# A mixed attention and gMLP trunk whose instructions are recorded and put in order by a model of the queues

## The chip, the cores and the metric

The kernel runs on one core of a Trainium2 chip. The metric is the device time of one execution in microseconds (us), lower is better. The core has engines that each work through a queue of their own strictly in order: TensorE (PE, with its weight loads shown apart as PEld), VectorE (DVE), ScalarE (ACT), GpSimd (POOL) and SyncE (SP), which here only starts transfers. An instruction at the head of a queue that waits for another engine holds up all that stand behind it.

## What is computed

One step of a four-layer trunk over 128 context tokens and 256 latent tokens (384 together), 2048 wide, in float32. Each layer is

```
x += gate * W_out( mixer(RMSNorm(x) * (1 + scale) + shift) * silu(z) )
(shift, scale, gate) = silu(cond) @ W_ada + b_ada
```

Layers 0 and 3 mix by windowed attention (16 heads of 128, 4 key heads), layer 1 by neighbourhood attention (16 heads with their own keys), layer 2 by a gMLP with 128x128 mixing in 16 groups. The attention layers also return their context keys and values.

## The kernel before

The large products are float32 products made of three: each operand is split into a high part (`H`, `hH`) and a remainder (`L`, `hL`), and `mm3` or `a_unit` issues H·hH, H·hL and L·hH into one PSUM bank. A weight block of 512 KB (`raw`, four buffers) is fetched by SP, ACT writes its `H` (three buffers), DVE its `L` (three buffers); that is `split`, line 159. One such block is a unit: `a_unit` has 24 products of 384 columns, `b_unit` 18 of 512 columns. 13,824 of the 16,872 products of the program are of these two kinds; the rest below calls them the long or main products.

Between them stand the short ones. `head` (line 812) handles one attention head: it turns q with six transposes (`trR`, 128 columns), forms the scores with three or so products of 128 columns and several of 256 or 384, and turns the probabilities with fourteen transposes before their product with the values. `k_gen` turns the keys. `pe_ada_unit` (line 1161) multiplies the modulation weights (`w_ada`) on PE in four column groups; the part of the modulation that DVE computes is `ada_one`, two reductions of 1024 columns a block (`vttr`, line 135).

The order in each queue is the order in which the Python code calls the engines. Where the main stream has finished a unit, `bg()` (line 302) lets generators advance by one step: a head, the square sums of q and k (`q_gen`, line 783), the next part of the modulation. So a step's transposes stand in the PE queue in a row, six to thirteen of them, and what a step does on DVE or ACT stands in one piece in their queues. The code keeps sums of estimated engine times (`pe_t`, `dve_t`, `act_t`), by which it decides whether a background step fits. `startup` (line 1211) interleaves the modulation of layer 0 with the first products.

Of the kernel before, what the change touches and what calls it, by code (L numbers as in the profile page):

```python
# [1 line left out]

# [6 lines left out]
F32R = mybir.dt.float32r  # L9
# [5 lines left out]
P = 128  # L15
# [21 lines left out]
    return bass.AP(ap.tensor, ap.offset, a)  # L37


class Net:  # L40
    def __init__(self, tc, pool, psum, dram, a):
        self.tc, self.nc, self.a = tc, tc.nc, a
        self.pe_t = self.dve_t = self.act_t = self.slot_t = 0.0
        self.lr = {}

        def t(name, cols, dt=F32):
            return pool.tile([P, cols], dt, name=name, tag=name)

        self.pool, self.seq = pool, 0
        self.hH, self.hL = t("hH", 16 * T, F32R), t("hL", 16 * T, F32R)  # L50
        self.pm, self.px = list(range(NPAIR)), []
        self.xt = [None] * NXP
        self.raw = [t(f"raw{i}", 1024) for i in range(NR)]
        self.H = [t(f"H{i}", 1024, F32R) for i in range(NH)]
        self.L = [t(f"L{i}", 1024, F32R) for i in range(NL)]
        self.araw = [None, None]
        self.cbc = t("cbc", 2048)
        self.qT = t("qT", 2 * T, F32R)
        self.aux = t("aux", 1536)
        self.junk = t("junk", 1024, BF16)  # L60
        self.ident = t("ident", P)
        self.identR = t("identR", P, F32R)
        self.ones = t("ones", P)
        self.mask = t("mask", 256, F32R)
        self.sel = t("sel", 4)
        self.spad = t("spad", 64)
        self.sT = t("sT", 32)
        self.normg = t("normg", 64)
        self.bada = t("bada", 192)
        self.sink = t("sink", 32)  # L70
        self.gk, self.gq = t("gk", P), t("gq", P)
        self.ada = [t(f"ada{i}", 96) for i in range(2)]
        self.accA = t("accA", 32)
        self.Av = [t(f"Av{i}", 32) for i in range(2)]
        self.st = [t(f"st{i}", 12) for i in range(6)]
        self.st_i = 0
        self.sm = [t(f"sm{i}", 24) for i in range(2)]
        self.cqs = [t(f"cq{i}", 12) for i in range(4)]
        self.c12 = t("c12", 12)
        self.bn = t("bn", 3 * 8 * 6)  # L80
        self.mv = t("mv", 6)
        self.bk = [psum.tile([P, 512], F32, name=f"bk{i}", tag=f"bk{i}") for i in range(8)]
        self.srow = dram.tile([2, D], F32, name="srow", tag="srow")
        self.xs = dram.tile([P, 16 * T], F32, name="xs", tag="xs")
        self.misc = []
        self.headq, self.heads, self.head_gap = [], [], 99
        self.heads_done = 0
        self.convq, self.conv_limit, self.conv_done, self.burst = [], 0, 0, 1
        self.ada_half, self.ada_wait, self.ada_hold = -1, 0, False
        self.units, self.uw, self.ua, self.ur, self.nd, self.pos = [], 0, 0, 0, 0, 0  # L90
        self.r_done = self.r_bank = None
# [341 lines left out]
    def setup(self):  # L433
        nc, a = self.nc, self.a
        self.scratch()
        craw, th = self.arow[:, :32], self.arow[:, 32:64]
        self.dma(craw, a["cT"])
        for i in range(NXP):
            self.xt[i] = self.new(f"pair{NPAIR + i}", 1536)
            self.dma(self.xt[i], a["xT"][:, i * 1536:(i + 1) * 1536])  # L440
        self.dma_upto(10)
        nc.scalar.dma_start(self.sel, a["sel"])
        self.act(th, craw, AF.Tanh, scale=0.5)
        make_identity(nc, self.ident)
        nc.vector.memset(self.ones, 1.0)
        nc.vector.memset(self.c12, -0.5)
        self.vstt(th, th, 1.0, craw, ALU.add, ALU.mult)
        self.vts(self.sT, th, 0.5, None, ALU.mult)
        self.pad_s()
        nc.scalar.dma_start(self.normg, a["normg"])  # L450
        nc.scalar.dma_start(self.bada, a["bada"])
# [929 lines left out]
    def run(self):  # L1381
        self.ada_layer = 0
        self.plan()
        self.setup()
        for l in range(4):
            self.ada_layer = l
            if l:
                self.ada_need(l, 0)
                self.make_A(l, 0, min(8, self.dve_chunks(l)))
            if l in (0, 3):  # L1390
                self.attn_layer(l, "win", l // 3)
            elif l == 1:
                self.attn_layer(l, "nat", 0)
            else:
                self.gmlp_layer(l)


# ---- launch: one core
# [111 lines left out]
```

## Time and profile before

| | us |
|---|---|
| median of 3 runs | 3072.14 |
| lowest, highest | 3071.66, 3074.43 |
| the profiled execution, its own time | 3072.06 |
| its span in the trace | 3070.2 |
| PE busy, weight loads busy | 3032.9, 2771.4 |
| DVE busy, ACT busy | 2174.0, 1271.6 |

The span is the stretch from the first to the last recorded instruction; 1.9 us of the execution's time lie outside of it. A product's recorded end is modelled and overlaps with the next one, so the busy share of PE says little; the distance from one product's start to the next one's says what it takes in the stream. By stage: 0 to 200 us is layer 0's startup, to about 660 us layer 0, to about 1430 us layer 1, to about 2530 us layer 2, and the rest layer 3.

### The profile page before, as it was taken

What the parts mean: (1) busy time and instruction counts of PE and PEld (TensorE: products, weight loads), DVE (VectorE), ACT (ScalarE), POOL (GpSimd) and SP (SyncE); (2) the same over time, 40 slices, a digit from 0 to 9 for tenths busy, and PEclk for the clock granted to TensorE, in tenths of its full rate; (3) what the DMA queues carried; (4) which work ended last, traced back from release to release, by engine and by line L of the source; (5) the groups of instructions that cost most, each with busy time, mean ns of one, the idle gap of its engine ahead of it and who ended that gap; (6) DMA issues with size and microseconds to landing.
All of it is one profiled execution on the core that took longest, in us unless ns stands there. A gap on an engine that the chain in (4) does not pass through costs nothing.

```text
span 3070.2 us, 45356 instructions
## 1 busy us (share of the span) xinstructions
PE 3032.9 (99%) x17616; PEld 2771.4 (90%) x17616; DVE 2174.0 (71%) x3604; ACT 1271.6 (41%) x2322; POOL 51.7 (2%) x29
## 2 busy tenths in 40 slices
PE   7999999999999999999999999999999999999999
PEld 4788899978989898998888999999999998999999
DVE  4478789868788888887988998445355566455654
ACT  4355555354444545534333222222232335455542
POOL 0000000000000000000000000000000000000000
PEclk9999999999999999999999999999999999999999
DMA  9756555976666666677777676444454474333343
GB/s 385 276 192 213 200 165 176 337 252 212 206 205 206 204 214 200 205 243 269 246 242 248 219 254 213 132 131 127 134 165 125 135 251 145 114 103 104 106 128 124
DMA packets 187361, 599.05 MB, mean 195 GB/s; under 512 B 21764, under 2 KB 47620, under 8 KB 187140
## 3 DMA queue, kind: packets, MB, share of 16 engines
q1 hardware_dynamic: 186712, 596.00, 58.3%
q8 instruction: 138, 2.26, 0.3%
q14 instruction: 79, 0.65, 0.1%
q10 hardware_dynamic: 432, 0.13, 0.0%
HBM read 580.31 MB, written 15.75 MB: 194 GB/s over the span
## 4 chain that ended last, share of the span: by engine, by line
PE 94%; DVE 2%; ACT 2%; issue 1%; DMA 1%; POOL 0%; SPq 0%; DVEq 0%; ACTq 0%; POOLq 0%
PE bk L109 92%; PE bk L118 3%; ACT junk L150 1%; DVE L L122 1%; DVE pair L133 1%; ACT H L150 0%; DVE pair L122 0%; POOL cq L165 0%; DMA pair<-i_w_ada 0%; ACT Pt L150 0%; DVE junk L137 0%; DMA pair<-i_xT 0%; DMA raw<-i_win_B 0%; DVE PLT L133 0%; DVE Pt L122 0%
## 5 line engine op out<-in xcount | busy, mean ns | idle before, releaser
L150 ACT ACTIVATE H<-raw 128x1024 fp32r<-128x1024 f32 x640 | 676.2, 1058 | 895.1 <-PE bk L109 805.4
L109 PE MATMUL bk<-hH,H 128*128 128x384 f32 x3072 | 1037.5, 338 | 3.4 <-DVE pair L122 3.4
L109 PE MATMUL bk<-hH,L 128*128 128x384 f32 x3072 | 1027.6, 334 | 0.0
L109 PE MATMUL bk<-hL,H 128*128 128x384 f32 x3072 | 1027.0, 334 | 0.0
L122 DVE TENSOR_TENSOR L<-raw,H 128x1024 fp32r<-128x1024 f32 x640 | 781.6, 1222 | 275.8 <-ACT H L150 267.3
L109 PE MATMUL bk<-L,hH 128*128 128x512 f32 x1536 | 600.9, 391 | 8.9 <-DVE L L122 8.9
L109 PE MATMUL bk<-H,hH 128*128 128x512 f32 x1536 | 607.5, 396 | 0.0
L109 PE MATMUL bk<-H,hL 128*128 128x512 f32 x1536 | 602.0, 392 | 0.3 <-DVE hL L122 0.3
L109 PEld LDWEIGHTS bk<-hH,H 128*128 128x128 f32 x3072 | 576.9, 188 | 13.7 <-issue 6.5
L109 PEld LDWEIGHTS bk<-hL,H 128*128 128x128 f32 x3072 | 577.1, 188 | 0.6
L109 PEld LDWEIGHTS bk<-hH,L 128*128 128x128 f32 x3072 | 576.7, 188 | 0.0
L109 PEld LDWEIGHTS bk<-L,hH 128*128 128x128 f32 x1536 | 289.5, 188 | 66.7 <-DVE L L122 11.0
L109 PEld LDWEIGHTS bk<-H,hL 128*128 128x128 f32 x1536 | 289.3, 188 | 65.3 <-DVE hL L122 3.8
L109 PEld LDWEIGHTS bk<-H,hH 128*128 128x128 f32 x1536 | 289.2, 188 | 64.6 <-issue 6.5
L137 DVE CUSTOM_DVE_ANT_0 junk<-araw,cbc,accA 128x1024 bf16<-128x1024 f32 x240 | 307.5, 1281 | 14.2 <-ACT junk L150 7.9
L137 DVE CUSTOM_DVE_ANT_0 junk<-araw,cbc,bada 128x1024 bf16<-128x1024 f32 x240 | 307.5, 1281 | 10.0 <-ACT junk L150 3.0
L133 DVE SCALAR_TENSOR_TENSOR pair<-bk,ada,pair 128x128 f32<-128x128 f32 x320 | 118.6, 413 | 202.4 <-PE bk L109 202.4
L150 ACT ACTIVATE pair<-bk 128x512 f32<-128x512 f32 (+3 forms) x156 | 86.9, 562 | 195.7 <-PE bk L109 172.4
L150 ACT ACTIVATE PLT<-bk 128x512 fp32r<-128x512 f32 (+2 forms) x63 | 34.0, 563 | 168.4 <-PE bk L118 150.2
L150 ACT ACTIVATE PTH<-bk 128x512 fp32r<-128x512 f32 (+2 forms) x74 | 37.0, 523 | 123.1 <-PE bk L118 87.9
L109 PE MATMUL bk<-pair,qT 128*128 128x384 f32 (+2 forms) x336 | 74.9, 332 | 0.0
L150 ACT ACTIVATE junk<-pair 128x128 bf16<-128x128 f32 x216 | 66.8, 309 | 13.4 <-DVE ada L137 5.9
(151 smaller groups left out, 2150.3 us busy)
## 6 DMA issues: line engine op xcount, KB each, us to landing
araw<-i_w_adaT SPq DMA_DIRECT2D x240, 512.0 KB, 3.8
pair<-i_w_ada SPq DMA_DIRECT2D x96, 512.0 KB, 8.2
raw<-i_win_B SPq DMA_DIRECT2D x96, 512.0 KB, 4.2
raw<-i_nat_B SPq DMA_DIRECT2D x96, 512.0 KB, 4.5
raw<-i_win_O SPq DMA_DIRECT2D x64, 512.0 KB, 3.7
raw<-i_gm_V SPq DMA_DIRECT2D x64, 512.0 KB, 4.6
raw<-i_gm_U SPq DMA_DIRECT2D x64, 512.0 KB, 4.5
raw<-i_gm_Z SPq DMA_DIRECT2D x64, 512.0 KB, 4.5
```

Of the source, the lines that this page charges most:

```text
L109: self.nc.tensor.matmul(out, lhsT, rhs, start=start, stop=stop, **kw)
L118: self.nc.tensor.transpose(out.bitcast(F32R), in_, self.identR)
L122: self.nc.vector.tensor_tensor(out=out, in0=in0, in1=in1, op=op)
L133: self.nc.vector.scalar_tensor_tensor(out=out, in0=in0, scalar=s, in1=in1, op0=op0, op1=op1)
L137: self.nc.vector.tensor_tensor_reduce(out=out, in0=in0, in1=in1, op0=op0, op1=op1, scale=1.0, scalar=scalar, accum_out=acc)
L150: self.nc.scalar.activation(out, in_, f, **kw)
```

## The change

A class `Rec` takes the place of the engine handles: while the kernel's code runs, it only notes each instruction with its operands. For each it finds what must come before it: data dependences by ranges of eight columns of a tile, order alone where both stand on one engine. Main products (those that read `hH` or `hL`) are chained and keep their recorded order, as do the products into one bank. Then `order` lays the instructions out in time by a model: once in recorded order, and three times by a list schedule in which PE takes the earliest recorded product that is ready and the other engines take the one whose result is due first. In that model a product that lasts over 100 ns is long; a weight load takes `LDW` = 108 ns and may begin once the load before it is over and the product before has started, and a product starts `LAG` = 56 ns after its load. Where no time is left for the next load, PE takes a long product before a short one. The real instructions are then issued in order of the modelled start. No product, no sum and no transfer is added or taken away, and the tiles are the same.

```diff
-        self.tc, self.nc, self.a = tc, tc.nc, a
+        self.tc, self.nc, self.a = tc, Rec(tc.nc), a
...
-        make_identity(nc, self.ident)
+        make_identity(nc.real, self.ident)
...
                 self.gmlp_layer(l)
+        self.nc.emit()
...
+    def cost(self, e, op, a, k):
+        n = self.cols(a[0] if a else k["out"])
+        if e == "tensor":
+            if op == "transpose":
+                d = 57
+            elif "tile_position" in k:
+                d = 128
+            elif a[2].dtype == F32R:
+                d = (n + 32) / 2.4 if n > P else 57
+            else:
+                d = max(4 * (n + 16) / 2.4, 224)
+            return d, d + 190
...
+    def add(self, e, op, a, k):
...
+        if e == "tensor" and any(s and s[0] in ("hH", "hL") for s in r):
+            if self.main is not None:
+                order.add(self.main)
+            self.main = i
+        self.ops.append((e, op, a, k))
...
+        self.long.append(d > 100)
...
+    SEM, LDW, LAG = 45, 108, 56
...
+    MARGIN = 250
+
+    def schedule(self, late):
...
+        key = [float(i) if self.eng[i] == 0 else late[i] for i in range(n)]
...
+            i = ready[e][0][1]
+            if e == 0:
+                if load + self.LDW + self.LAG > t and not self.long[i]:
+                    i = min((i for _, i in ready[0] if self.long[i]), default=i)
...
+                load = max(load + self.LDW, last)
+                t = last = max(t, load + self.LAG)
+            if e in (1, 2) and wait[e]:
+                end, hold = t + self.dur[i], None
+                for est, j in wait[e]:
+                    if est < end and late[j] < end and late[j] < late[i] and (hold is None or est < hold):
+                        hold = est
+                if hold is not None:
+                    free[e] = hold
+                    continue
...
+    def order(self, passes=3):
+        start, done = self.in_order()
+        for _ in range(passes):
+            start, done = self.schedule(self.due(start))
+        return sorted(range(len(self.ops)), key=lambda i: (start[i], i))
+
+    def emit(self):
+        for i in self.order():
+            e, op, a, k = self.ops[i]
+            getattr(getattr(self.real, e), op)(*a, **k)
```

Three places show what moves. In the rows below, a number behind a name tells buffers apart, `x4` stands for four equal instructions in a row, and all of the change's instructions carry line 314, since they are issued there.

The first is PE in layer 3, some 130 us before the end, where one head's probabilities (`PLT_792`) are turned into banks 5 and 6, and the product with the values of the head before (`PTH_793` with `pair7`) goes into bank 7. Before:

```order
L109 MATMUL bk2_115<-hL_66,H0_71 128x384
L109 MATMUL bk2_115<-hH_65,L0_74 128x384
L118 MATMUL bk5_118<-identR_82,PLT_792_23153 128x128 x4
L118 MATMUL bk6_119<-identR_82,PLT_792_23153 128x128 x3
L109 MATMUL bk7_120<-PTH_793_23207,pair7_700_20540 128x128
L109 MATMUL bk7_120<-PLT_795_23266,pair7_700_20540 128x128
```

And with the change:

```order
L314 MATMUL bk2_115<-hL_66,H0_71 128x384
L314 MATMUL bk2_115<-hH_65,L0_74 128x384
L314 MATMUL bk5_118<-identR_82,PLT_792_918 128x128 x2
L314 MATMUL bk3_116<-hH_65,H1_72 128x384
L314 MATMUL bk5_118<-identR_82,PLT_792_918 128x128 x2
L314 MATMUL bk3_116<-hL_66,H1_72 128x384
L314 MATMUL bk6_119<-identR_82,PLT_792_918 128x128 x2
L314 MATMUL bk3_116<-hH_65,L1_75 128x384
L314 MATMUL bk6_119<-identR_82,PLT_792_918 128x128
L314 MATMUL bk7_120<-PTH_793_919,pair7_700_826 128x128
L314 MATMUL bk3_116<-hH_65,H1_72 128x384
```

Seven transposes in a row have become pairs with a long product between them. Over the whole program the 1,104 transposes stood in 142 runs of 6 to 13 and now stand in 625 runs, 479 of two and 146 of one. Runs of modulation products were 61 and are 69.

At the same place ACT copies the turned probabilities out of banks 5 and 6 (`PTH`, `PLT`) and takes the exponentials of the next head (`Pt_794`) out of banks 7 and 4. Before:

```order
L150 ACTIVATE hH_65<-pair3_749_21949 128x384
L150 ACTIVATE H2_73<-raw2_69 128x1024
L150 ACTIVATE PLT_795_23266<-bk5_118 128x512
L150 ACTIVATE PLT_795_23266<-bk6_119 128x384
L150 ACTIVATE Pt_794_23221,sm0_104<-bk7_120,sm0_104,cq3_109 128x128
L150 ACTIVATE Pt_794_23221,sm0_104<-bk7_120,sm0_104,cq3_109 128x384
L150 ACTIVATE Pt_794_23221,sm0_104<-bk4_117,sm0_104,cq3_109 128x384
```

With the change:

```order
L314 ACTIVATE H2_73<-raw2_69 128x1024
L314 ACTIVATE PTH_793_919<-bk5_118 128x512
L314 ACTIVATE PTH_793_919<-bk6_119 128x384
L314 ACTIVATE Pt_794_920,sm0_104<-bk7_120,sm0_104,cq3_109 128x128
L314 ACTIVATE Pt_794_920,sm0_104<-bk7_120,sm0_104,cq3_109 128x384
L314 ACTIVATE Pt_794_920,sm0_104<-bk4_117,sm0_104,cq3_109 128x384
L314 ACTIVATE H0_71<-raw3_70 128x1024
L314 ACTIVATE sm0_104<-sm0_104,sink_90 128x3
L314 ACTIVATE PLT_795_921<-bk5_118 128x512
```

The exponentials have moved ahead of the copies of `PLT_795`.

The second place is DVE at the first group of heads in layer 1, where q is normed (`q_gen`): a sum (`st2`), from which POOL forms `cq0`, and twelve multiplications by `cq0`, among the splits (`L0`, `L1`, `L2`) of the main stream's weights. Before:

```order
L122 TENSOR_TENSOR L1_75<-raw2_69,H1_72 128x1024
L127 TENSOR_SCALAR st2_100<-st1_99 128x12
L133 SCALAR_TENSOR_TENSOR pair9_297_6149<-pair9_297_6149,cq0_106,gq_92 128x128 x12
L122 TENSOR_TENSOR L2_76<-raw3_70,H2_73 128x1024
L122 TENSOR_TENSOR pair10_301_6243<-pair9_297_6149,pair12_300_6242 128x512 x3
L122 TENSOR_TENSOR L0_74<-raw0_67,H0_71 128x1024
```

With the change (`ISA` is a modulation reduction and, with one operand, the reading of its sum):

```order
L314 TENSOR_TENSOR L2_76<-raw3_70,H2_73 128x1024
L314 ISA junk_80,accA_95<-araw1_294_420,cbc_77,bada_89 128x1024
L314 ISA accA_95 128x1
L314 TENSOR_TENSOR L0_74<-raw0_67,H0_71 128x1024
L314 TENSOR_SCALAR st2_100<-st1_99 128x12
L314 ISA junk_80,accA_95<-araw0_298_424,cbc_77,bada_89 128x1024
L314 ISA accA_95 128x1
L314 ISA junk_80,accA_95<-araw0_298_424,cbc_77,bada_89 128x1024
L314 ISA accA_95 128x1
L314 TENSOR_TENSOR L1_75<-raw1_68,H1_72 128x1024
L314 SCALAR_TENSOR_TENSOR pair9_297_423<-pair9_297_423,cq0_106,gq_92 128x128 x11
L314 TENSOR_TENSOR L2_76<-raw2_69,H2_73 128x1024
```

Two reductions and a split have come between the sum and the multiplications, and the two splits that stood behind the multiplications stand ahead of the sum. The other three groups of the layer are alike.

The third place is SP at the very start, where it fetches x (`pair9` to `pair12`), the modulation weights in 512 KB blocks and the first weights of the main stream (`raw0`, `raw1`). Before:

```order
L102 DMA PTH_3_125<-i_cT 128x32
L102 DMA pair9_5_128<-i_xT 128x1536
L102 DMA pair10_6_130<-i_xT 128x1536
L102 DMA pair11_7_132<-i_xT 128x1536
L102 DMA pair12_8_134<-i_xT 128x1536
L102 DMA pair0_9_136<-i_w_ada0 128x1024
...
L102 DMA pair5_14_146<-i_w_ada0 128x1024
L102 DMA raw0_67<-i_win_B 128x1024
L102 DMA pair6_15_149<-i_w_ada0 128x1024
L102 DMA pair7_16_151<-i_w_ada0 128x1024
L102 DMA raw1_68<-i_win_B 128x1024
```

With the change:

```order
L314 DMA pair9_5_127<-i_xT 128x1536
L314 DMA pair10_6_128<-i_xT 128x1536
L314 DMA pair0_9_131<-i_w_ada0 128x1024
L314 DMA PTH_3_125<-i_cT 128x32
L314 DMA pair11_7_129<-i_xT 128x1536
L314 DMA pair1_10_132<-i_w_ada0 128x1024
L314 DMA pair12_8_130<-i_xT 128x1536
...
L314 DMA pair7_16_138<-i_w_ada0 128x1024
L314 DMA araw0_17_139<-i_w_ada0 128x1024
L314 DMA raw0_67<-i_win_B 128x1024
L314 DMA araw1_19_145<-i_w_ada0 128x1024
```

The first main weights have moved behind nine blocks of the modulation, and two of these go ahead of the last quarter of x. In the same stretch DVE now multiplies the first two column blocks of x by the norm (`Pt<-pair9,bk7`, twice) before the modulation is added up, where it did that behind it.

## Rows read from the trace of the kernel before

**Rows 1.** The page: busy time of PE and the other engines, and the chain that ended last.

```profile
PE 3032.9 (99%) x17616; PEld 2771.4 (90%) x17616; DVE 2174.0 (71%) x3604; ACT 1271.6 (41%) x2322; POOL 51.7 (2%) x29
...
PE 94%; DVE 2%; ACT 2%; issue 1%; DMA 1%; POOL 0%; SPq 0%; DVEq 0%; ACTq 0%; POOLq 0%
```

**Rows 2.** Waits of PE: instruction, what it waited for, total us, times, longest.

```profile
PE bk L109 <- DVE L L122: 8.9, 5, 1.9
PE bk L109 <- DVE Pt L122: 2.2, 1, 2.2
PE bk L109 <- ACT Pt L150: 2.2, 1, 2.2
PE bk L118 <- DVE PTH L142: 2.0, 2, 1.0
```

**Rows 3.** Timeline of PE in layer 1: start, us, instruction, count; two runs of transposes.

```profile
805.82 0.40 PE L109 MATMUL bk<-H,hL 128*128 128x512 f32 x1
806.05 0.71 PE L118 MATMUL bk<-identR,PH 128*128 128x128 f32 x7
806.60 0.68 PE L118 MATMUL bk<-identR,pair 128*128 128x128 f32 x6
...
807.41 0.39 PE L109 MATMUL bk<-L,hH 128*128 128x512 f32 x1
...
1005.50 0.71 PE L118 MATMUL bk<-identR,PH 128*128 128x128 f32 x7
...
1006.35 0.39 PE L109 MATMUL bk<-L,hH 128*128 128x512 f32 x1
```

**Rows 4.** Timeline of PE in layer 0: one short product between long ones, twice.

```profile
504.73 0.22 PE L109 MATMUL bk<-mask,identR 128*128 128x128 f32 x1
504.79 0.73 PE L109 MATMUL bk<-pair,qT 128*128 128x384 f32 x3
505.35 0.22 PE L109 MATMUL bk<-mask,identR 128*128 128x128 f32 x1
```

**Rows 5.** First group of layer 1: timelines of PE and DVE, then one window (PEclk: granted clock).

```profile
732.66 0.39 PE L109 MATMUL bk<-H,hH 128*128 128x512 f32 x1
734.94 0.50 PE L109 MATMUL bk<-L,hH 128*128 128x512 f32 x1 [1.90 <-DVE L L122]
...
730.51 3.24 DVE L133 SCALAR_TENSOR_TENSOR pair<-pair,cq,gq 128x128 f32<-128x128 f32 x12 [2.38 <-POOL cq L165]
...
733.00:740.00 7.00, 5.10 (x16) 4.02 (x16) 6.96 (x11) 2.88 (x4) 0.00 (x0) 0.76 0.40 112
1203.00:1209.00 6.00, 4.10 (x14) 2.92 (x13) 6.00 (x13) 3.41 (x5) 0.00 (x0) 0.79 0.29 91
```

**Rows 6.** The head in layer 3: timelines of PE and ACT, and one window.

```profile
2943.49 0.33 PE L109 MATMUL bk<-PTH,pair 128*128 128x128 f32 x1 [2.16 <-ACT Pt L150]
...
2941.37 0.98 ACT L150 ACTIVATE PLT<-bk 128x512 fp32r<-128x512 f32 x2 [4.29 <-PE bk L118]
...
2943.00:2948.00 5.00, 4.50 (x24) 4.51 (x25) 3.23 (x7) 4.69 (x12) 0.00 (x0) 0.66 0.09 20
```

**Rows 7.** The start: timeline of PE, and one window of 10 us.

```profile
13.09 1.08 PE L109 MATMUL bk<-pair,spad 128*32 128x256 f32 x8 [13.09 <-DMA pair<-i_w_ada]
...
26.15 0.61 PE L109 MATMUL bk<-sel,PTH 128*128 128x4 f32 x4 [0.51 <-ACT PTH L150]
28.97 1.08 PE L109 MATMUL bk<-araw,spad 128*32 128x256 f32 x8 [2.21 <-DVE Pt L122]
...
30.84 0.80 PE L109 MATMUL bk<-H,hH 128*128 128x512 f32 x1
...
10.00:20.00 10.00, 6.37 (x43) 2.81 (x43) 5.04 (x10) 4.71 (x9) 0.00 (x0) 1.00 1.02 419
```

**Rows 8.** Layer 0 as one window; DVE's modulation reductions by line.

```profile
200.00:660.00 460.00, 457.85 (x2977) 415.52 (x2976) 373.84 (x686) 224.87 (x489) 11.35 (x5) 1.00 0.64 225
...
L137 DVE CUSTOM_DVE_ANT_0 junk<-araw,cbc,accA 128x1024 bf16<-128x1024 f32 x240 | 307.5, 1281 | 14.2 <-ACT junk L150 7.9 <-DMA araw<-i_w_adaT 2.0
```

202 lines of the change are left out of this document (added).

## The prediction, made before the changed kernel was timed

> **What bounds the kernel now.** I read the page first: PE is busy for 99% of the span and 94% of the chain that ended last is PE's [rows 1]. So the kernel is one stream of products, and a change of order can move the time in two ways only: by what a product takes in the stream, which is the distance from its start to the next start, and by the places where PE stands waiting. I then read the waits of PE. Apart from the start they are few: 8.9 us in five waits for DVE's `L`, and 2.2, 2.2 and 2.0 us for other results [rows 2], some 20 us in all with smaller ones. DVE and ACT have slack in the mean (71% and 41% busy), so where they end nothing is decided. Last I read the timeline of PE around short products, since the change is about them.
>
> **What a short product takes, and what splitting the runs costs.** A long product of 512 columns starts 0.23 us after the one before it (805.82 to 806.05). A run of seven transposes between long ones moves the second long product behind it to 1006.35, from a first transpose at 1005.50: 0.85 us, less 0.23 for the long one that lies in between, 0.62 us for seven. A run of thirteen, from 806.05 to 807.41, leaves 1.13 us by the same reckoning [rows 3]. Six more transposes cost 0.51 us, 0.085 each, and the first seven cost 0.62 and not 0.60: a run pays about 0.025 us more than its transposes, at its end, where a long product's weights are loaded. By this a single transpose costs 0.11 us and a pair 0.195. No transpose stood alone before, but another short product did: the 128-column `mask` product between 384-column ones. From one to the next there are 0.62 us (504.73 to 505.35) with three long products in them [rows 4]. These take three quarters of 0.227 us each, 0.51 together, so one short product between long ones costs 0.11 us, though its successor is recorded 0.06 us after it and the delay only shows behind that one. I read it so: the load of the product after a short one starts no earlier than the short one, and a short product is too brief to cover it, whoever its neighbours are. The change's model lets the long product go on 57 ns behind the short one; this trace does not.
>
> The transposes stood in 142 runs and now stand in 625. 483 more ends of runs at 0.025 us are **+12.1 us**, all on PE's stream, with no cover. Products of 128 columns other than transposes cost 0.11 us in either order: nothing. Eight more breaks around modulation products are two such load delays each, about 0.1 us: **+1 us**, and 2.5 at most if each costs 0.3.
>
> [...]
>
> **What the waits give back.** First, layer 1. At the end of each of the four groups' q products DVE waits 2.38 us for POOL's `cq` with twelve multiplications to do, 3.24 us, and the split `L` that PE needs stands behind them; PE's products are 2.28 us apart instead of 0.23 [rows 5]. In the new DVE queue two reductions (1.28 us each [rows 8]) and a split lie between the sum and the multiplications, some 3.7 us, in which POOL is done; and two splits stand ahead of it all. I take all four waits as gone: 4 x 2.05 = **-8.2 us**. [...] Second, layer 3. PE waits 2.16 us for the exponentials, which ACT does behind the copies of `PLT` (0.98 us); the clock is 0.66 over the next 5 us, 1.7 us lost [rows 6]. The exponentials now stand first: **-3.9 us**. Third, two waits of a run of transposes for DVE's copies, 2.0 us [rows 2]; with the run pulled apart the copies have time: **-2.0 us**.
>
> Fourth, the start. PE begins at 13.09 us, waits at 28.97 for 2.21 us for DVE, which multiplies x only when the modulation is summed, and reaches the first main product at 30.84 [rows 7]. The modulation's chain is bound by its eight blocks and the norm, not by the first block: that the first comes several us earlier is worth nothing by itself. But the block of main weights that stood ahead of the seventh and eighth is now behind them, 512 KB at 419 GB/s, 1.25 us [rows 7], and the early multiplication takes the 2.2 us away: **-3.5 us**. Bounds: 0, if DVE's later steps are what holds the first main product, and -5, if the earlier blocks also free PE for the norm's products. From the second block on PE was fully busy though transfers ran at the limit, so I let the gain stand.
>
> What is late next at these places is nothing that the trace shows; where every queue is put in another order, some waits may be new. Their bound from below is 0, from above the old waits again, 16 us; I put 0 into the sum since PE now runs about 0.05 us behind the model at each short run, so that the other engines are ahead of what the model gave them.
>
> **The sum.** 3072.06 (the profiled execution; the median is 3072.14) + 12.1 + 1.0 - 8.2 - 3.0 - 3.9 - 2.0 - 3.5 = 3064.6, rounded down to **3064 us**, -0.26%, since the end of a run read from the first seven transposes is 0.02 to 0.025. A measurement of this kernel can tell about 0.2%, 6.1 us, from no change, so this stands just on the faster side of 3066.
>
> **The rivals.**
>
> *Half of the waits stay.* The change's order follows modelled times, and a queue in order passes a wait on to whatever stands behind it. If the layer 3 wait, the start and the two copies stay, 9.4 us do not come back: 3073 us, no change. For it: the waits for DVE at the end of the startup, some 4 us, hang on the order of main products that is kept. Against it: the four waits in layer 1 have a plain cause that the new order takes away.
>
> *DVE's splits come late in layer 0.* There DVE is busy for 374 of 460 us [rows 8]. The model fills it with modulation reductions as soon as their data are there, unless a split is due. Before, at most 7.5 us of DVE's work stood between two splits in layer 0; now, counted from the order with durations as in rows 8, seven stretches have 8 to 9.5 us, with up to five reductions of 1.36 us with their sums. PE has two units in hand, 48 long products of 0.17 us, 8.2 us, and the short ones between them. Where the split before such a stretch was itself no more than on time, PE waits a us or so and the lower clock adds 1.7 [rows 6]: 7 x 2.9 = 20 us, **3084 us**, slower. It decides at a lead of about 1.3 us: with that much in hand no stretch is felt. Against it: there are three buffers for `L`, and before, DVE kept ahead of PE in this layer at the same load.
>
> *The loads are hidden after all.* Then each transpose takes 0.06 us, as the first of a run does (504.73 to 504.79 for the `mask` product [rows 4]), and not 0.089: 1,104 x 0.03 = 33 us, and some 260 of the other 128-column products, which now have a long neighbour, 0.05 us each, 13 us. With the term of 12.1 gone: 3064 - 12 - 46 = **3006 us**. Against it stand rows 3 and 4.
>
> **How the numbers follow.** The forecast has 0.62: 3054 to 3071, about 0.47 of it below 3066. Half of the waits staying has 0.20 (3069 to 3078). Late splits 0.13, 0.11 of it above 3078.3. Hidden loads 0.05. So faster by over 0.2%: 0.47 + 0.05 = 0.52; within: 0.15 + 0.18 + 0.02 = 0.35; slower: 0.13 with the upper end of the waits that stay. The range of 3052 to 3079 leaves out the hidden loads, most of the late splits and the tail of the forecast, under 0.2.
>
> **What would show it.** In the profile of the changed kernel: a single transpose between long products with the second product behind it 0.11 us late, a pair 0.195; if these are 0.06 and 0.12, the first term is wrong. Waits of PE for DVE's `L` in layer 1 gone, with the clock at full level there; the wait for ACT's exponentials in layer 3 gone; the first 512-column product at about 27.3 us. PE waiting for DVE in layer 0, with reductions right before the split, would show the slower rival. The prediction falls if new waits of over 15 us in sum appear or if the runs cost nothing more than before.

## The result, and the profile with the change

With the change the kernel takes **3093.02 us** (median of 4 runs, 3084.99 to 3094.74), beside 3071.92 us for the kernel before on the same chip: a ratio of 1.0062 between the mean times (95% interval 1.0043 to 1.0080), slower by 0.6%. The forecast was 3064 us, and the range ended at 3079. The profiled execution took 3092.39 us, with a span of 3090.3 us. One of the four runs, 3084.99 us, had a granted clock of 1.000 over its span where the others had 0.997 to 0.998, and no trace of it was kept.

The page, busy time and chain, answers to [rows 1]:

```profile
PE 3052.9 (99%) x17616; PEld 2776.6 (90%) x17616; DVE 2144.7 (69%) x3604; ACT 1278.2 (41%) x2322; POOL 54.6 (2%) x29
...
PE 93%; DMA 3%; DVE 2%; issue 1%; ACT 0%; SPq 0%; DVEq 0%; ACTq 0%
```

PE is busy 20.0 us longer for the same 17,616 products (the count that the page has, where 16,872 was stated above), and the share of transfers in the chain has gone from 1% to 3%. The waits of PE (what it waited for, total us, times, longest) answer to [rows 2]:

```profile
PE bk L314 <- DVE spad L314: 11.1, 1, 11.1
PE bk L314 <- DVE pair L314: 7.4, 7, 2.7
PE bk L314 <- DVE sm L314: 6.3, 10, 3.1
PE bk L314 <- ACT hH L314: 3.9, 4, 1.7
PE bk L314 <- DVE L L314: 2.4, 2, 1.8
...
```

The first is the start. The five waits for `L` are two, neither of them in layer 1; the wait for the exponentials is not in the list. But waits for `sm` (the maxima of the scores), `hH` and `pair` have come.

**Where the time came from.** The main products keep their order, so the start of the n-th of them can be set beside its start in the kernel before. I counted them in the two traces (change minus before, in us):

| main product | place | difference |
|---|---|---|
| 1st | start | -1.9 |
| 500th | about 180 us | +0.7 |
| 2250th | end of layer 0 | +3.3 |
| 2500th | in layer 1, behind the boundary | +6.5 |
| 5250th | end of layer 1 | +5.9 |
| 6250th | layer 2, about 1560 us | +6.7 |
| 7000th | layer 2, about 1720 us | +15.6 |
| 11250th | end of layer 2 | +15.6 |
| last | | +20.2 |

The largest piece, 8.9 us, lies in 160 us of layer 2, where the forecast expected nothing. Timelines of DVE and PE there, and one window (PE busy, then the other engines; the decimal before the last two numbers is the granted clock):

```profile
1655.22 1.22 DVE L314 TENSOR_TENSOR L<-raw,H 128x1024 fp32r<-128x1024 f32 x1
1660.35 1.28 DVE L314 CUSTOM_DVE_ANT_0 junk<-araw,cbc,accA 128x1024 bf16<-128x1024 f32 x1 [3.91 <-DMA cbc<-srow]
...
1662.43 1.28 DVE L314 CUSTOM_DVE_ANT_0 junk<-araw,cbc,accA 128x1024 bf16<-128x1024 f32 x1 [0.78 <-DMA cbc<-srow]
...
1663.63 1.22 DVE L314 TENSOR_TENSOR L<-raw,H 128x1024 fp32r<-128x1024 f32 x1
...
1664.91 0.50 PE L314 MATMUL bk<-L,hH 128*128 128x512 f32 x1 [1.76 <-DVE L L314]
...
1717.97 2.00 PE L314 MATMUL bk<-aux,pair 128*128 128x128 f32 x6 [2.67 <-DVE pair L314]
...
1716.00:1726.00 10.00, 7.90 (x36) 7.42 (x37) 9.36 (x16) 1.47 (x3) 0.00 (x0) 0.83 0.66 199
```

A modulation reduction (`junk`) stands at the head of DVE's queue and waits 3.91 us for the broadcast of the condition vector (`cbc`). Nobody needs the reduction soon. Behind it stands the split `L` (1663.63), and PE waits for that. DVE has lost its lead, has only short gaps from here on (five more waits for weight blocks, 2.4 us in sum), and 50 us later PE waits 2.67 us for another of its results; then the granted clock is 0.83 over 10 us.

The same pattern in layer 1, behind a weight block of the modulation, and at the boundary of layers 0 and 1, on ACT, behind the masks:

```profile
1242.98 1.28 DVE L314 CUSTOM_DVE_ANT_0 junk<-araw,cbc,bada 128x1024 bf16<-128x1024 f32 x1 [3.73 <-DMA araw<-i_w_adaT]
...
1245.52 0.29 DVE L314 TENSOR_REDUCE sm<-bk 128x1 f32<-128x128 f32 x1
...
1245.86 0.33 PE L314 MATMUL bk<-ck,qT 128*128 128x128 f32 x1 [3.10 <-DVE sm L314]
...
655.02 0.42 ACT L314 ACTIVATE mask<-pair 128x256 fp32r<-128x256 f32 x1 [1.76 <-DMA pair<-i_masks]
...
656.78 0.50 PE L314 MATMUL bk<-H,hH 128*128 128x512 f32 x1 [1.67 <-ACT hH L314]
...
656.00:664.00 8.00, 7.22 (x24) 5.68 (x25) 6.43 (x19) 5.45 (x12) 0.00 (x0) 0.79 0.00 1
```

What DVE waited for before its modulation reductions, in the whole program (us, times), and how long the broadcast takes from issue to landing:

```profile
  DMA araw<-i_w_adaT: 37.9, 49
  DMA cbc<-srow: 15.4, 9
...
DMA to landing us min/median/max: 3.9/6.2/10.5
```

In the kernel before, the first of these rows read 4.8 us in 6, and there was none for `cbc`. The broadcast has not become slower (4.2 to 8.5 us, median 6.3, before), and the weight blocks land 0.6 us later in the median (4.4 us, 3.8 before). Most of the new idle time is therefore that the reductions stand closer behind their transfers. The change's model gives a block of 512 KB 3.3 us (0.7 + 1.33 + 1.3) where nothing else moves.

SP's transfers here land later than that: 4.4 us in the median for the modulation's weight blocks (3.3 to 10.2 with those of the start), and 6.2 us for the broadcast.

### The profile page after: what moved, and what is told of

Its sections match the earlier page's. It is cut to its first block, busy times and chain, and to the rows that moved or that the text cites. A ratio compares the mean times of both kernels' runs of the same rounds, so it can differ in the third digit from the quotient of the medians.

```text
span 3090.3 us, 45480 instructions
## 1 busy us (share of the span) xinstructions
PE 3052.9 (99%) x17616; PEld 2776.6 (90%) x17616; DVE 2144.7 (69%) x3604; ACT 1278.2 (41%) x2322; POOL 54.6 (2%) x29
## 4 chain that ended last, share of the span: by engine, by line
PE 93%; DMA 3%; DVE 2%; issue 1%; ACT 0%; SPq 0%; DVEq 0%; ACTq 0%
PE bk L314 93%; DMA araw<-i_w_adaT 2%; DVE junk L314 1%; DVE L L314 1%; DMA raw<-i_win_B 0%; DVE pair L314 0%; DMA pair<-i_xT 0%; DMA pair<-i_masks 0%; ACT Pt L314 0%; DMA sel<-i_sel 0%; DVE bn L314 0%; DMA pair<-i_gvec 0%; ACT H L314 0%; DVE sm L314 0%; DVE Pt L314 0%
## 5 line engine op out<-in xcount | busy, mean ns | idle before, releaser
L314 PE MATMUL bk<-L,hH 128*128 128x512 f32 x1536 | 607.6, 396 | 2.5 <-DVE L L314 2.4
L314 DVE SCALAR_TENSOR_TENSOR pair<-bk,ada,pair 128x256 f32<-128x256 f32 x320 | 119.6, 413 | 230.8 <-PE bk L314 230.5
L314 PE MATMUL bk<-pair,qT 128*128 128x384 f32 (+2 forms) x336 | 87.2, 343 | 1.9 <-DVE sm L314 1.9
L314 ACT ACTIVATE Pt<-bk,sm,cq 128x384 f32<-128x384 f32 (+1 forms) x96 | 56.6, 596 | 65.1 <-DVE sm L314 65.1
L314 DVE SCALAR_TENSOR_TENSOR PLT<-Pt,sm,PH 128x128 fp32r<-128x128 f32 x144 | 69.7, 525 | 17.0 <-ACT PH L314 8.5
L314 ACT ACTIVATE PH<-Pt,sm 128x128 fp32r<-128x128 f32 x144 | 67.9, 535 | 24.3 <-DVE sm L314 24.3
```

The source lines that it names most:

```text
L314: getattr(getattr(self.real, e), op)(*a, **k)
```

## The experiments

The theory after the result: **three things**. The broken runs of transposes cost about what the forecast says. The gains of the other queues come as forecast. And new waits, forecast as 0, come because the model lands transfers too early, so that instructions without hurry stand at the head of an in-order queue and wait. All runs were timed beside the kernel before, which gave 3071.9 to 3072.3 us.

### First four: what the parts are worth

**e1** takes the preference for long products out of `schedule`:

```diff
-                    if e == 0 and not any(self.long[i] for _, i in ready[0]):
-                        t = max(t, load + self.LDW + self.LAG)
...
-                if load + self.LDW + self.LAG > t and not self.long[i]:
-                    i = min((i for _, i in ready[0] if self.long[i]), default=i)
```

> The change without its preference for long products: PE takes the earliest recorded product that is ready, so the transposes stand in 143 runs again (142 before the change, 625 with it); the other queues are still put in order by the model. Theory: the changed kernel's +20 us are two separate things, some 13 us of run ends on PE (483 at 0.027 us) and new waits that come from the order of the other queues. Then this takes back only the first: 3093 - 13 = 3080 us, with PE's new waits behind DVE (spans about 1246, 1665 and 1690 us) still there. Rival A, that the pulled-apart runs also make the waits: these go too, 3065 us. Rival B, that the run ends are cheap and the waits are all: 3090 us or more.

Measured: **3077.64 us** (1.0016, 1.0007 to 1.0025), 15.4 us less than with the change. DVE's idle time before the reductions stays (45.2 and 15.3 us), and so does the loss in layer 2. The theory, with a run end somewhat dearer.

**e2** lets data arrive later in the model, at both places where it sets a transfer's end:

```diff
-                done[i] = max(dma + 1300, t + self.lat[i])
+                done[i] = max(dma + 1300, t + self.lat[i]) + self.LAND
...
+    LAND = 4000
```

> The change with one number added: in the model every transfer's data arrive 4.0 us later. Theory: PE's new waits stand behind instructions of DVE and ACT that wait at the head of their queue for a transfer that the model lands too early (DVE idle for transfers before modulation reductions: 53 us in 58 waits with the change, 4.8 us in 6 before it; ACT 1.8 us for the masks at the boundary of layers 0 and 1). With the later landing DVE's idle time for these falls under 16 us, PE's waits at 656, 1246, 1665 and 1690 us are gone with the lower clock behind them: 3093 - 13 = 3080 us, the transposes still in some 620 runs. Rival, that the new waits come from due times in general (DVE's queue too full ahead of splits): they stay, 3090 to 3096 us.

Measured: **3083.85 us** (1.0036, 1.0023 to 1.0048), 9.2 us less than with the change, of 13 expected. DVE's idle time for transfers before the reductions falls from 53.3 us to this one row:

```profile
DVE junk L315 <- DMA araw<-i_w_adaT: 0.3, 1, 0.3
```

Layer 2 now loses nothing. The due-times rival falls. The wait at the boundary of layers 0 and 1, which I had expected to go, stays with 1.12 us (1.67 with the change), so the masks were only a part of it. What else was left over is a set of short waits for `sm` (14, 4.8 us), taken up below.

**e3** makes both edits.

> Both edits together: no preference for long products, and transfers that land 4.0 us later in the model. If the two causes are separate their gains add up: 3093 - 13 - 13 = 3067 us, faster than the kernel before by 0.15%. If the waits come from the order in general: 3080 us. If the run ends were what made the waits: same as without the preference for long products alone, within 2 us.

Measured: **3066.31 us** (0.9980, 0.9971 to 0.9989). The two gains add up (15.4 and 9.2 make 24.6; measured 26.7), so the causes are separate as far as the spread of the change's own runs lets one tell.

**e4** leaves every queue but PE's in recorded order:

```diff
+    KEEP = ('vector', 'scalar', 'gpsimd', 'sync')
...
+        if e in self.KEEP:
+            if e in self.prev:
+                order.add(self.prev[e])
+            self.prev[e] = i
         self.ops.append((e, op, a, k))
```

> Only PE is put in order by the model; DVE, ACT, POOL and SP keep the recorded order. Theory: the kernel before plus the run ends: 3072 + 13.5 = 3086 us, with the four waits for L in layer 1 and the wait for the exponentials in layer 3 still there, and no new waits at 1246 and 1665 us. Rival, that PE's own order brings the new waits: they are there too, 3095 us or more. Run ends that cost nothing: 3073 us.

Measured: **3096.64 us** (1.0078, 1.0065 to 1.0091), 10 us over the theory and at the rival's figure. The long waits of layer 2 and at 1246 us are not there, but PE's order brings waits of its own, while those for `L` shrink and that for the exponentials in layer 3, expected to stay, is gone, as they would if PE comes later:

```profile
PE bk L320 <- DVE sm L320: 6.5, 17, 0.4
PE bk L320 <- ACT pair L320: 3.8, 8, 0.8
...
PE bk L320 <- DVE L L320: 2.0, 5, 1.3
```

Seventeen waits for `sm`, none over 0.4 us, with DVE in its old order: a second fault of the model, not the transfers. What the 10 us are made of in full is not shown.

### Which transfer, and PE's order

**e5** gives the 4.0 us to the modulation's blocks and the vector `cbc` alone, **e12** to `cbc` alone:

```diff
+        mod = op == "dma_start" and a[0].tensor.name.startswith(("araw", "cbc"))
+        self.land.append(4000 if mod else 0)
```

> The change with the later landing (4.0 us in the model) for two kinds of transfers alone: the modulation's weight blocks and the broadcast of its condition vector. All others, the main weights among them, land as the change models them. Theory: it is DVE's modulation reductions, early in the queue for data that aren't there, that hold up the splits, so this gives nearly all that the later landing of every transfer gave (3083.9 us); the wait for the masks at the boundary of layers 0 and 1 stays with its clock drop, 2 to 3 us: 3086 us. Rival, that the landing of the main weights is what counts: 3091 to 3095 us.

> The change with the later landing (4.0 us) for one kind of transfer alone, the broadcast of the modulation's condition vector; the modulation's weight blocks land as the change models them. Theory: the long waits of layer 2 (1665, 1690 and about 1720 us, 8.9 us lost there) begin behind the vector, the wait at 1246 us behind a weight block. So layer 2 is made good and layer 1 is not: 3093 - 9 = 3084 us. Rival, that the weight blocks hold the splits in layer 2 as well: 3089 to 3093 us.

Measured: **3081.68 us** (e5; 1.0029, 1.0018 to 1.0041) and **3082.13 us** (e12; 1.0034, 1.0021 to 1.0046). The vector alone gives 10.9 us. In e12 DVE still stands idle for 32.3 us in 38 waits for the weight blocks, and beside e5 that costs nothing measurable: these waits are short (2.3 us at most), and that most of them find a lead in front of PE is my reading. I had expected the wait at 1246 us to stay whole in e12; it is 1.70 us there instead of 3.10, and 0.38 where every transfer lands later (e2, at 1243.56). So the weight blocks are the smaller part.

**e6** keeps PE in recorded order (`KEEP = ('tensor',)`) with all transfers 4.0 us later.

> PE keeps the recorded order to the last product; the other queues are ordered by the model with transfers that land 4.0 us later. Against the run with no preference for long products and the same landing (3066.3 us), only PE's order differs. Theory: what is left there of waits of PE for DVE's maxima of the scores (13 waits, 5.0 us in sum) comes from PE taking a head's products early, and goes: 3062 us. Rival, that the model's order of PE is worth what it moves: 3068 us or more.

Measured: **3061.95 us** (0.9965, 0.9953 to 0.9978), as the theory had it, but for another reason: 12 waits for `sm` (4.6 us) are still there. One of them, on PE and on DVE:

```profile
2630.89 0.22 PE L321 MATMUL bk<-mask,identR 128*128 128x128 f32 x1
2631.49 0.80 PE L321 MATMUL bk<-pair,qT 128*128 128x384 f32 x3 [0.38 <-DVE sm L321]
...
2631.14 0.29 DVE L321 TENSOR_REDUCE sm<-bk 128x1 f32<-128x128 f32 x1 [2.66 <-PE bk L321]
2632.14 0.56 DVE L321 TENSOR_REDUCE sm<-bk 128x1 f32<-128x384 f32 x1 [0.71 <-PE bk L321]
```

And DVE in the kernel before, for a head in the same layer:

```profile
2642.99 1.22 DVE L146 TENSOR_REDUCE sm<-bk 128x1 f32<-128x128 f32 x3 [2.61 <-PE bk L109]
```

A head's scores are several products into one bank. The maximum of the first 128 columns now stands, in the issued program, ahead of further products into the same bank, and the first of these waits until the maximum is done: it starts 0.60 us behind the `mask` product, where it took 0.06 [rows 4]. In the kernel before, three maxima follow each other (2642.99, `x3`) with no product waiting for the first. `Rec` notes ranges of eight columns, so to it the two have nothing to do with each other.

So the waits in this trace (12 of them for `sm`, 0.4 us at most, 4.6 us in sum) agree with a dependence by the whole bank and not by the columns; what the products would do without them was not tried.

**e7** raises the model's `MARGIN` from 250 to 1000 on top of e3.

> No preference for long products, transfers 4.0 us later, and the margin by which a result of another engine must be done before PE's product is taken, raised from 0.25 to 1.0 us in the model. Theory: the 13 waits of 0.4 us for DVE's maxima are products that the model takes within the margin of their release; with 1.0 us they are taken later and no longer wait: 3066.3 - 4 = 3062 us. Rival, that the margin only shifts the model's clock and not the order: 3066 us, the 13 waits as they are.

Measured: **3071.39 us** (0.9993, 0.9984 to 1.0002): a miss. The waits for `sm` stay (15, 5.8 us, where e3 has 13, 5.0 us), and 5 us are lost, 1.6 of them between the 5500th and the 6000th main product, at the boundary of layers 1 and 2. A margin can't mend a dependence that isn't noted.

**e8** puts `LAND` at 8000 on top of e1.

> No preference for long products, and transfers that land 8.0 instead of 4.0 us later in the model. The trace has 0.7 us of DVE's idle time for the modulation's transfers left at 4.0 us. Theory: there is nothing more to gain, and reductions that come later still have slack: 3066 us, within 2 us of the run with 4.0 us. Rival, that more of the splits or the boundaries still wait in the shadow of transfers: 3062 us. If the reductions now run out of slack, they pile up at the ends of the layers: 3070 us or more.

Measured: **3168.41 us** (1.0310, 1.0296 to 1.0324). The third case, and far larger than thought. At the end of layer 1 the modulation of layer 2 isn't finished, and PE stands still. PE's waits for ACT's `pair` come to 43.5 us in 8; the longest, 21.8, lies inside layer 1, and the chain before it leads from 1251.70 to 1262.85 through DVE, with three reductions (3.77 us) and a transfer of one of their weight blocks (4.04 us). The longest of all:

```profile
1508.51 0.80 PE L311 MATMUL bk<-H,hH 128*128 128x512 f32 x1 [35.90 <-ACT hH L311]
```

### The second fault, and the price of a run end

**e9** is e6 with one edit in `span`, and **e10** is e3 with the same:

```diff
+        if name[:2] == "bk":
+            return name, 0, 512, ap.tensor.name
         lo = int(ap.offset) % max(p[0][0], 1)
```

> PE in recorded order, transfers 4.0 us later in the model, and one more edit: what reads a PSUM bank depends on the whole bank, not on the columns that it reads. Theory: the waits of PE for DVE's maxima (12 of 0.4 us, 4.6 us in sum, with PE in recorded order) come from a maximum of the first columns that the model puts ahead of the bank's last product; the program then makes the product wait for it, which the model doesn't know. With the whole bank noted the maximum comes behind the products as recorded, the 12 waits are gone: 3062.0 - 5 = 3057 us. Rival, that PE waits there for something else that DVE does late: 3062 us, the waits under another name.

> The same edit on the model's PE order without the preference for long products (3066.3 us before the edit, with 13 waits for the maxima, 5.0 us). Theory: 3061 us, and some 4 us above the run with PE in recorded order, as without the edit. Rival, that the difference between the two PE orders came from the maxima: the two are now equal, within 2 us.

Measured: **3054.44 us** (e9; 0.9945, 0.9932 to 0.9957) and **3058.19 us** (e10; 0.9957, 0.9945 to 0.9970), 7.5 and 8.1 us less than without the edit. Waits for `sm` are gone in both; the rows of e9 behind that of the start (the first of them belongs to layer 0's startup too):

```profile
PE bk L323 <- DMA pair<-i_w_ada: 5.0, 4, 2.2
PE bk L323 <- DVE pair L323: 4.0, 4, 1.6
PE bk L323 <- ACT hH L323: 1.9, 4, 0.8
PE bk L323 <- ACT PLT L323: 1.2, 1, 1.2
PE bk L323 <- DVE PH L323: 0.5, 3, 0.2
PE bk L323 <- ACT PTH L323: 0.5, 1, 0.5
```

The gain is larger than the recorded waits (4.6 and 5.0 us). The one above is recorded with 0.38 us, while its product starts 0.54 us late (0.60 us behind `mask` where it took 0.06): if all 12 are like it, that is an estimate of 6.5 us.

**e13** is e10 with the preference for long products put back, that is, the change with both faults mended.

> The change with both mends of the model (transfers 4.0 us later, readers of a bank depend on the whole bank) and with its preference for long products: the transposes stand in 624 runs again, where the run without the preference (3058.2 us) has 144. The waits that the change brought are gone in both, so that the difference is the price of 480 run ends. Theory, from the starts in the trace (three pairs of transposes take 0.06 us more than one run of six, 0.03 us for each further end): 3058.2 + 14 = 3072 us. Rival, that a run end costs 0.036 us as the 17.5 us between the two runs with 4.0 us alone would have it: 3076 us. If the preference hides loads in part: under 3068 us.

Measured: **3074.18 us** (1.0005, 0.9996 to 1.0014), 16.0 us over e10. The lists of PE's waits in the two differ by less than 1 us, so this is the price of pulling the runs apart, half way between the theory's 3072 and the rival's 3076. There are 624 against 144 runs of transposes, **0.033 us for each further end** if these alone pay. But the preference also pulls apart the other products of at most 128 columns: counted in the two traces, e13 has 387 runs of them and e10 256. All short products together stand in 968 runs against 357, which makes 0.026 us for each of 611 further ends. The changed kernel's own trace shows the price in layer 0, seven transposes as three pairs and one single, and the weight load (PEld) behind the single one:

```profile
417.03 0.28 PE L314 MATMUL bk<-identR,PLT 128*128 128x128 f32 x2
417.15 0.46 PE L314 MATMUL bk<-H,hH 128*128 128x512 f32 x1
417.45 0.28 PE L314 MATMUL bk<-identR,PLT 128*128 128x128 f32 x2
417.57 0.47 PE L314 MATMUL bk<-L,hH 128*128 128x512 f32 x1
417.88 0.28 PE L314 MATMUL bk<-identR,PLT 128*128 128x128 f32 x2
418.00 0.47 PE L314 MATMUL bk<-H,hL 128*128 128x512 f32 x1
418.30 0.22 PE L314 MATMUL bk<-identR,PLT 128*128 128x128 f32 x1
418.36 0.45 PE L314 MATMUL bk<-H,hH 128*128 128x512 f32 x1
418.65 0.40 PE L314 MATMUL bk<-L,hH 128*128 128x512 f32 x1
...
418.31 0.19 PEld L314 LDWEIGHTS bk<-H,hH 128*128 128x128 f32 x1
```

From 417.03 to 418.65 are 1.62 us, with four long products of 0.227 us in them: 0.71 us for seven transposes, where a run of seven takes 0.62 [rows 3]: 0.03 us for each of three further ends. A pair takes 0.20 us (417.45 to 417.88, less 0.227), the single 0.12. The load for the long product behind the single transpose starts at 418.31, that transpose at 418.30.

**e11** puts `LAND` at 2000 in e9.

> PE in recorded order with the whole bank noted, and transfers that land 2.0 instead of 4.0 us later in the model. In the trace the blocks of the modulation land 4.4 us and the condition vector 6.2 us after their issue (medians), where the model without the addition gives 3.3 us. Theory: 2.0 us are enough for the blocks and not for the vector, so that some of the waits in layer 2 come back: 3057 + 4 = 3061 us. Rival, that 2.0 us cover it: 3057 us, as with 4.0.

Measured: **3054.59 us** (0.9944, 0.9931 to 0.9958): the rival. DVE waits a little for transfers (3.2 us for `cbc`, 9.0 for the blocks), and the time doesn't show it. Between 2 and 4 us the number doesn't matter (3054.59 and 3054.44 us); at 0 it costs what e2 gives back (9.2 us), and at 8 more (3168.41 us in e8, where e3 has 3066.31).

### The start

**e14** is e9 with SP too in recorded order; **e15** keeps SP's recorded order up to the 500th main product only (the cut is against e14).

```diff
-        if e in self.KEEP:
+        if e in self.KEEP and (e != "sync" or self.mains < 500):
```

> PE and SP both keep the recorded order; DVE, ACT and POOL are ordered by the mended model. Against the run with PE alone kept (3054.4 us), only the order of the transfers differs. Theory: in the stretch from 30 to 110 us the transfers run at their limit (share 0.99 with the change), so an earlier first main product is only waited for later, and the order of the transfers moves no total there: 3054 us, within 2 us, with the 500th main product no later than in the kernel before. Rival, that the new order of the transfers delays what layer 0 needs (the 500th main product is 1.6 us later than before there): 3051 us. If the order of the transfers carries gains elsewhere: 3060 us or more.

Measured: **3140.92 us** (1.0223, 1.0209 to 1.0237), by the number the third case, but 81 us beyond it, far more than all that e9 gains (18 us). DVE does the reductions at other times than SP's recorded order reckons with, so SP waits for it longer before modulation blocks (`ada`, `accA`; 17.1 us at most, 7.1 in the kernel before), and the main weights stand behind. SP's own waits and two of PE's:

```profile
SPq L323 <- DVE ada L323: 487.4, 104, 17.1
SPq L323 <- DVE accA L323: 445.9, 98, 17.1
...
PE bk L323 <- DVE L L323: 35.1, 21, 4.4
PE bk L323 <- ACT H L323: 26.7, 9, 8.6
```

That queues which hand buffers to each other should be ordered together is what this one run says (3140.92 us, where e9 has 3054.44). At the start, though, the recorded order was better: the 500th main product comes 1.4 us earlier than in the kernel before, and 1.8 us later in e9.

> As the run with PE kept and both mends of the model (3054.4 us), and SP keeps the recorded order up to the 500th main product; behind it the model orders the transfers. Theory: the model's order of the transfers at the start costs what the trace has there (500th main product at +1.6 us against the kernel before, at -1.7 with SP recorded), and the part behind it is as without the edit: 3054.4 - 3.3 = 3051 us. Rival, that what is gained by the 500th product is given back in waits by the end of layer 0: 3054 us. If SP's recorded order starves what stands behind the 500th product: 3058 us or more.

Measured: **3054.02 us** (0.9937, 0.9924 to 0.9951). In the profiled executions e15 is 2.0 us ahead of e9 at the 500th main product and at the end; the medians differ by 0.4 us, less than their spread. Open.

## Why the prediction was wrong, step by step

| step | forecast | measured | from |
|---|---|---|---|
| run ends | +12.1 | +16.0 | e13 less e10 |
| breaks around modulation products | +1.0 | at most +3.8 | e10 less e9, where other parts of PE's order differ too |
| gains of the other queues, with the start | -20.6 | -17.9 | e9 less before |
| new waits | 0 | +18.8 | change less e13 |
| sum | -7.5 | +20.7 | the change: +21.1 |

The four differences lead from the kernel before to the change, so that their sum must come out near it and proves nothing by itself. The last one carries the spread of the change's own runs: its interval reaches some 6 us to either side. Between the two traces it is 18.0 us.

**The step that failed is the last term.** The forecast set new waits to 0, bounded them by the old ones (16 us), and gave as the reason that PE would run late against the model, so that the other engines were ahead. That says nothing of transfers: the broadcast takes 6.2 us from issue to landing with the change and 6.3 before. Nor does it cover a dependence that the model doesn't have: the text of the change has data dependences by ranges of eight columns, and the forecast did not ask whether the program keeps them by the bank. I had read DVE's waits for PE's sake but not DVE's own waits for transfers in the kernel before (4.8 us), and I had not set the model's 3.3 us beside the landing times that the profile gives, 3.8 to 6.3 us for such blocks. The landing times are on the page, the 4.8 us in the list of DVE's waits. Of the 18.8 us, the later landing alone gives 9.2 (e2), and the whole bank, added to it, the other 9.7 (e13 against e2). So the model landed its transfers too early and missed a dependence, and the two cost about the same.

**Run ends: mechanism right, size off.** In the row above the load of the product behind a short one starts no earlier than the short one (418.31 and 418.30), as the forecast read it, and pulling runs apart costs time. A pair takes 0.20 us (forecast 0.195), a single 0.12 (0.11). The term came out 3.9 us short, and two reasons fit. The end of a run was read as 0.025 us from a difference of 0.62 and seven times 0.085, where a hundredth of a microsecond is a third of the result, and the rows under e13 give 0.03. And the forecast put the other short products at nothing "in either order", while their runs were pulled apart too (389 with the change, 250 before); with these counted, an end costs 0.026 us. No run tells the two apart. The rival of hidden loads falls.

**Modulation breaks.** e10 has 73 of these runs and e9 has 61; 3.8 us for 12 would be 0.3 us each, the upper bound that the forecast named. But PE's four waits for `hH` come to 4.2 us in e10 and to 1.9 in e9, so up to 2.3 of the 3.8 us can be waits. The price of a break stays open between 0.1 and 0.3 us.

**The gains came.** In e9, against the kernel before and counted by main products, the stretch between the 2500th and the 5250th in layer 1 gains 12.4 us (forecast 11.2 for the four waits and the clock), layer 3 2.5 us (forecast 3.9), and the rest of layer 0 2.7 us (forecast 2.0 for the two copies). No run shows the 3.0 us that the sum takes off for the clock in layer 1: what the runs show is a granted clock of 0.76 and 0.79 in two windows before [rows 5] and of 1.00 in both in e9, with the 12.4 us for waits and clock together. The windows at the three places, at full clock and with PE never idle, answer to [rows 5, rows 6]:

```profile
733.00:740.00 7.00, 7.00 (x33) 5.80 (x32) 7.00 (x18) 3.02 (x5) 0.91 (x1) 1.00 0.66 194
1203.00:1209.00 6.00, 6.00 (x28) 4.99 (x27) 5.96 (x9) 1.35 (x2) 0.00 (x0) 1.00 0.86 264
2943.00:2948.00 5.00, 5.00 (x35) 5.00 (x34) 2.40 (x6) 3.01 (x6) 0.00 (x0) 1.00 0.34 105
```

**The start came half, and went again.** The first 512-column product starts at 28.96 us, with the change, forecast 27.3, before 30.84 [rows 7]. By the 500th product nothing is left. The stretch from 30 to 110 us, before and with the change:

```profile
30.00:110.00 80.00, 80.00 (x579) 54.90 (x568) 40.10 (x68) 28.93 (x43) 0.00 (x0) 0.99 0.91 362
...
30.00:110.00 80.00, 79.92 (x567) 54.09 (x566) 40.98 (x70) 28.06 (x41) 0.00 (x0) 1.00 0.99 397
```

With the change the transfers have no slack left there (share 0.99). Whether that is the whole reason stays open with e15.

**The rivals.** Layer 0 shows no wait of PE for `L`: the slower rival named the wrong layer and the wrong cause. Its core, a split behind modulation reductions, is what happened in layer 2, but by a reduction that waited, not by one too many. That half of the waits stay did not come: 17.9 of 20.6 us were given back once the model was mended.

## What to carry to other kernels

Before an instruction order is left to a model, compare each latency in it with the landing times and durations that the profile shows (here 3.3 us in the model, 4.4 and 6.2 measured), and its rules of dependence with the waits that the program will really carry (12 for `sm` in e6 that the model didn't have). An instruction without hurry that waits at the head of a queue holds up what stands behind it (3.91 us for `cbc` here, ahead of a split), so it should stand well behind its data, but not so far that it misses its own deadline (35.90 us of PE's time in e8). Two mended lines of the model, with PE left in its recorded order (e9), turned a loss of 0.6% into a gain of 0.55%.

## What was not expected of the hardware

The landing time of the modulation's weight blocks (512 KB each) spreads from 3.3 to 10.2 us within one execution, and the broadcast of one row to all partitions takes 6.2 us in the median where a plain weight block takes 4.4. DVE stood idle 32.3 us for weight blocks in e12 without any measurable cost (3082.13 us, 3081.68 in e5), while 12.4 us less of it for the broadcast (15.4 to 3.0) gave 10.9 us back. So it is not the sum of the waits that counts here; that it is the lead of the engine where they fall is my reading, and no run measures that lead.
